# A decoder trunk on one core: the norms' sums on VectorE, the odd norm's row inside the first query, mixing behind the scores

## The chip, the core and the metric

The kernel runs on one core of a Trainium2 chip. The core has five engines that run side by side and meet through semaphores: TensorE (matmuls, written PE), VectorE (DVE), ScalarE (ACT), GpSimd (POOL) and SyncE (SP, which here only starts DMAs). The metric is the time of one execution on the device in microseconds; it is given as the median of several runs.

## The reference

A trunk of four pre-norm residual layers over 256 tokens of 1024 channels, in float32, and a final norm. Cut to what is computed:

```python
def rmsnorm(x, g):
    y = x * rsqrt(mean(x * x, axis=-1) + 1e-6)
    return y * g

def trunk(x):                                  # 1 x 256 tokens x 1024
    h = x
    # even layer: gated conv of width 3 (512 channels) beside pooling over 2/4/8/16 positions (512)
    h = h + even_mixer(rmsnorm(h, mix_g[0]))   # w_in 1024 x 2048, w_out 1024 x 1024
    h = h + conv_ffn(rmsnorm(h, ffn_g[0]))     # w_in 1024 x 5632, w_out 2816 x 1024
    # odd layer: 8 heads of forgetting attention, 8 of MoBA with a T5 bias; w_in 1024 x 3080, w_out 1024 x 1024
    h = h + odd_mixer(rmsnorm(h, mix_g[1]))
    h = h + conv_ffn(rmsnorm(h, ffn_g[1]))
    return rmsnorm(h, final_g)

def conv_ffn(h):
    u, g = split(h @ w_in)                     # 2816 each
    return (silu(causal_dwconv3(u) + b) * g) @ w_out
```

## The kernel before

**Layout.** Activations stand transposed: `h` is 128 partitions x 8 chunks of 1024 channels x 256 tokens. All weights are read once, in blocks of 128x1024 float32, by DMAs that SyncE starts into eight staging buffers `st`. A block is split into two parts of reduced precision: ScalarE casts `hi` (L141), VectorE subtracts and keeps `lo` (L142). The split blocks stand in rings of seven buffers, six blocks ahead of their use, so that the cast of a block waits until TensorE is through with the block seven before it. Every product is the sum of three: `hi` with `x_hi`, `hi` with `x_lo`, `lo` with `x_hi` (L290 to L292), or, in the FFN, one matmul of 512 columns (L314, both parts of `x` side by side) and one of 256 (L315).

**Stages.** Even layer, FFN 0, odd layer, FFN 1, final norm. A `boundary` between two layers (L383) closes the product in four blocks b=0..3, adds each to `h` (L381), and splits `h` times the norm's gain into `hg` (ScalarE L209, VectorE L210); the split has a high priority, since the next layer's first products read it. The norm's factor, one number per token, is multiplied in later, behind the products. For it `Stats.feed` squares each block of `h` (ScalarE L225, two buffers `sq`), GpSimd adds the squares up (`sqs` L230, `tot` L235), `columns` sums over partitions by two matmuls with ones into `pst` (L238), VectorE makes `var` of it (L252) and GpSimd raises it to -1/2 (`rcol` L254: a column, one number per partition). `rows` turns `rcol` by two transposes (L244) and ScalarE copies them as `rrow` (L247).

**FFN.** 22 chunks f of 128 channels. The in-product of f gives `zu` and `zg`; `added` copies them into `zs` (three buffers); `gate` multiplies with `rrow` (L549), does the convolution, the SiLU and the product `y` (L556), which is split into `y_h` and `y_l`. The out-product of f comes some chunks later, the last two of FFN 0 in the boundary behind it. For f=0 u and g alternate. `columns` stands between u and g of f=1; `rows`, with the gates of f=0 and 1 right behind it, between u and g of f=2.

**Odd layer.** `values(0)` makes the values of the first heads and the forget gates' inputs in four PSUM banks `pv` of the pool psA, all that it has, with `columns` ahead of the last chunk; ScalarE and VectorE scale them by `rcol` (`va` L642 and L643, `xg` L641). Then come `rows` and `rq`, and a loop over eight pairs of heads i: queries of i (`zq`, 24 matmuls, and in their middle `turn(i-2)`, six transposes of the probabilities `pr`), `score(i-1)` (12 matmuls of 64 rows, `ps_s`), keys of i (`zk`, 24 matmuls, and in their middle `mix(i-2)`, four matmuls of 64 columns into `po`). VectorE makes logits `lg` of the scores, ScalarE the exponentials, VectorE divides (L732 to L734); `po` is split into `yoh` and `yol`. Behind the loop stand the out-products `odd_add`, 24 matmuls each, among which the last pairs are turned, scored and mixed.

**What sets the order.** TensorE's order is that of the program. ScalarE's and VectorE's is fixed too when the program is built, by a scheduler that goes by priorities, except in the start and in the final norm, where it is that of the program. Each engine takes its instructions strictly in that order.

## Time and profile before

| | |
|---|---|
| median of 3 runs | 576.18 us (575.69 to 576.53) |
| profiled execution | 576.41 us, its span 574.7 us |
| mean granted clock of TensorE | 0.995 |
| busy: TensorE, VectorE, ScalarE, GpSimd | 98%, 78%, 60%, 11% |

The span is what the trace covers, from the first instruction to the last; 1.7 us of the profiled execution lie around it. A row of a timeline has the start, the time of its instructions taken together (neighbours that read alike are one row, with their count behind an x), the engine, the line, and in brackets how long the engine stood idle ahead of it and what it waited for. TensorE's matmuls overlap: what one costs is the distance between two starts, not the time in its row.

### The profile page before, as it was taken

How to read it: one execution, taken by the hardware profiler on the slowest of the kernel's cores; microseconds unless marked ns; L12 is line 12 of the kernel's file. 1: busy time of each engine (PE TensorE's matmuls, PEld its weight loads, DVE VectorE, ACT ScalarE, POOL GpSimd, SP SyncE). 2: the span in 40 equal slices, each digit the busy share in tenths (PEclk: the TensorE clock that was granted, in tenths of full speed). 3: DMA queues.
4: the chain of work that ended last, by engine and by line, in shares of the span. 5: the costliest groups of instructions: out<-in, count | busy, mean ns of one | idle time of the engine just before them, and what ended most of it. 6: DMA issues, size and time to landing. Idle time of an engine off the chain costs nothing.

```text
span 574.7 us, 9941 instructions
## 1 busy us (share of the span) xinstructions
PE 563.5 (98%) x3774; PEld 510.9 (89%) x3774; DVE 449.8 (78%) x776; ACT 346.0 (60%) x611; POOL 64.7 (11%) x81
## 2 busy tenths in 40 slices
PE   8999999999999999999899999999999999999995
PEld 7999988999999999999889999998888888888883
DVE  6999697987788778779648888488977778887752
ACT  6764476665655555557557666566755556555532
POOL 1542031000000000004001335031000000000000
PEclk9999999999999999999899999999999999999999
DMA  8965736566566656654665543437556655655001
GB/s 307 404 234 198 251 106 219 195 210 186 184 188 192 198 185 187 190 182 134 226 194 167 194 130 120 159 112 257 174 192 182 188 192 182 200 181 196 2 0 74
DMA packets 30080, 104.44 MB, mean 182 GB/s; under 512 B 3632, under 2 KB 3904, under 8 KB 30032
## 3 DMA queue, kind: packets, MB, share of 16 engines
q1 hardware_dynamic: 28944, 100.87, 53.9%
q0 software_dynamic: 944, 2.68, 1.6%
q8 instruction: 29, 0.48, 0.3%
q10 hardware_dynamic: 144, 0.26, 0.1%
q14 instruction: 19, 0.16, 0.1%
HBM read 102.73 MB, written 1.07 MB: 181 GB/s over the span
## 4 chain that ended last, share of the span: by engine, by line
PE 57%; issue 34%; DVE 4%; ACT 2%; POOL 2%; DMA 1%; SPq 0%; POOLq 0%; ACTq 0%; DVEq 0%
PE zu L314 8%; PE zg L314 7%; PE zu L315 4%; PE zg L315 4%; PE ta L291 3%; PE ta L290 3%; PE ta L292 3%; PE pv L633 2%; PE zk L290 2%; PE acc L290 2%; DVE lo L142 2%; PE acc L291 1%; PE acc L292 1%; PE zq L290 1%; PE zq L291 1%
## 5 line engine op out<-in xcount | busy, mean ns | idle before, releaser
L142 DVE TENSOR_TENSOR lo<-st,hi 128x1024 fp32r<-128x1024 f32 (+2 forms) x186 | 228.4, 1234 | 74.6 <-ACT hi L141 73.3
L141 ACT CAST hi<-st 128x1024 fp32r<-128x1024 f32 (+2 forms) x186 | 192.2, 1039 | 119.2 <-PE acc L291 32.1
L314 PE MATMUL zu<-hg,hi 128*128 128x512 f32 x352 | 125.6, 394 | 0.6 <-DVE hg L210 0.6
L314 PE MATMUL zg<-hg,hi 128*128 128x512 f32 x352 | 125.6, 394 | 0.0
L315 PE MATMUL zu<-hg,lo 128*128 128x256 f32 x352 | 98.6, 280 | 0.0
L315 PE MATMUL zg<-hg,lo 128*128 128x256 f32 x352 | 98.5, 280 | 0.0
L314 PEld LDWEIGHTS zu<-hg,hi 128*128 128x128 f32 x352 | 66.1, 188 | 15.9 <-DVE hg L210 1.3
L314 PEld LDWEIGHTS zg<-hg,hi 128*128 128x128 f32 x352 | 66.2, 188 | 14.9
L315 PEld LDWEIGHTS zu<-hg,lo 128*128 128x128 f32 x352 | 66.2, 188 | 0.7
L315 PEld LDWEIGHTS zg<-hg,lo 128*128 128x128 f32 x352 | 66.2, 188 | 0.0
L291 PE MATMUL acc<-y_l,hi 128*128 128x256 f32 x176 | 49.5, 281 | 0.0
L290 PE MATMUL acc<-y_h,hi 128*128 128x256 f32 x176 | 49.5, 281 | 0.0
L292 PE MATMUL acc<-y_h,lo 128*128 128x256 f32 x176 | 49.3, 280 | 0.0
L323 ACT CAST y_h<-y 128x256 fp32r<-128x256 f32 x44 | 17.7, 406 | 39.6 <-DVE y L556 39.6
L291 PE MATMUL ta<-lo,y_h 128*128 128x512 f32 x88 | 34.7, 394 | 0.0
L290 PE MATMUL ta<-hi,y_h 128*128 128x512 f32 x88 | 34.7, 394 | 0.0
L292 PE MATMUL ta<-hi,y_l 128*128 128x512 f32 x88 | 34.5, 393 | 0.0
L290 PEld LDWEIGHTS acc<-y_h,hi 128*128 128x128 f32 x176 | 33.1, 188 | 0.8
L291 PEld LDWEIGHTS acc<-y_l,hi 128*128 128x128 f32 x176 | 33.3, 189 | 0.0
L292 PEld LDWEIGHTS acc<-y_h,lo 128*128 128x128 f32 x176 | 33.2, 188 | 0.0
L401 ACT ACTIVATE t<-zs,vec 128x256 f32<-128x256 f32 x44 | 26.4, 600 | 11.0 <-DVE zs L549 10.9
L549 DVE TENSOR_TENSOR zs<-zs,rrow 128x512 f32<-128x512 f32 x44 | 30.2, 691 | 1.2
(217 smaller groups left out, 1160.6 us busy)
## 6 DMA issues: line engine op xcount, KB each, us to landing
st<-in_ff_in SPq DMA_DIRECT2D x88, 512.0 KB, 4.1
st<-in_ff_out SPq DMA_DIRECT2D x44, 512.0 KB, 4.3
st<-in_od_qk SPq DMA_DIRECT2D x16, 512.0 KB, 4.5
st<-in_ev_in SPq DMA_DIRECT2D x10, 512.0 KB, 7.4
st<-in_ev_out SPq DMA_DIRECT2D x8, 512.0 KB, 4.3
st<-in_od_out SPq DMA_DIRECT2D x8, 512.0 KB, 3.4
first<-in_first SPq DMA_DIRECT2D x7, 388.0 KB, 6.5
st<-in_od_vf SPq DMA_DIRECT2D x4, 520.0 KB, 3.6
```

The lines of the kernel that those rows point to most:

```text
L141: nc.scalar.copy(hi[:, s:e], st[:, s:e])
L142: nc.vector.tensor_sub(lo[:, s:e], st[:, s:e], hi.bitcast(F32)[:, s:e])
L290: nc.tensor.matmul(o, wh, xh, start=start, stop=False, skip_group_check=skip)
L291: nc.tensor.matmul(o, wh, xl, start=False, stop=False, skip_group_check=skip)
L292: nc.tensor.matmul(o, wl, xh, start=False, stop=stop, skip_group_check=skip)
L314: nc.tensor.matmul(z, wh, x[:, k], start=first, stop=False, skip_group_check=True)
L315: nc.tensor.matmul(z[:, 1, :], wl, x[:, k, 0, :], start=False, stop=last, skip_group_check=True)
L323: nc.scalar.copy(hi, src)
L401: nc.scalar.activation(t, u, AF.Identity, scale=col(w0 + 2), bias=bias)
L549: nc.vector.tensor_mul(zs, zs, rrow[:, None, :].to_broadcast([P, 2, T]))
L633: nc.tensor.matmul(o[:, :e - s], x[y], w[z][:, kk * c + s:kk * c + e], start=k == y == z == 0, stop=k == NK - 1 and y == 1)
```

## The change

- The sums of squares, `sqs` (three per norm) and `tot`, go from GpSimd to VectorE, in all four norms that have them.
- In the FFN `columns` stands behind g of f=1, and `rows` with the two gates behind g of f=2.
- In the odd layer `rows` and `rq` go into the middle of the first pair's query product.
- `mix(i-2)` stands right behind `score(i-1)`, and the keys' 24 matmuls run on without a break. In the tail `odd_add(1)` stands ahead of the last score.
- At the start the dummy operand of the warming matmuls is one column, broadcast; one of the first DMAs is started by ScalarE's queue, and ScalarE's first square comes behind it.
- In the final norm the division by 1024 goes into the squares' scale, and ScalarE's half of the first output (`send_left(0)`) stands behind the square of the last product.

```diff
--- before.py
+++ after.py
@@ -173,11 +173,11 @@
     place = {b[0]: i for i, b in enumerate(blocks)}
 
 
-    dummy = const.tile([P, T], F32, name="dummy")
+    dummy = const.tile([P, 1], F32, name="dummy")
     nc.vector.memset(dummy, 0.0)
     pw_ = psA.tile([P, 512], F32, tag="ps", name="pwarm")
     for _ in range(WARM):
-        nc.tensor.matmul(pw_[:, :T], dummy[:, :P], dummy, start=True, stop=True)
+        nc.tensor.matmul(pw_[:, :T], dummy.to_broadcast([P, P]), dummy.to_broadcast([P, T]), start=True, stop=True)
     vec = const.tile([P, V_N], F32, name="vec")
     ident = const.tile([P, P], F32, name="ident")
     make_identity(nc, ident)
@@ -211,8 +211,6 @@
                                        op0=ALU.mult, op1=ALU.subtract)
 
     hg = new_hg()
-    warm = const.tile([P, 1], F32, name="warm")
-    nc.scalar.activation(warm, ones, AF.Square)
     class Stats:
 
 
@@ -227,12 +225,12 @@
                 self.sum = sq
             else:
                 s = nrm.tile([P, 2, T], F32, tag="sqs", name="sqs")
-                nc.gpsimd.tensor_add(s, self.sum, sq)
+                nc.vector.tensor_add(s, self.sum, sq)
                 self.sum = s
 
         def columns(self, ps):
             tot = nrm.tile([P, T], F32, tag="tot", name="tot", bufs=1)
-            nc.gpsimd.tensor_add(tot, self.sum[:, 0, :], self.sum[:, 1, :])
+            nc.vector.tensor_add(tot, self.sum[:, 0, :], self.sum[:, 1, :])
             self.p = ps.tile([P, 512], F32, tag="ps", name="pst")
             for i in range(2):
                 nc.tensor.matmul(self.p[:, i:i + 1], tot[:, i * P:(i + 1) * P], ones, start=True, stop=True)
@@ -265,7 +263,9 @@
     rc = const.tile([P, PAD], F32, name="rc")
     for k in range(NK):
         for s, e in ((0, LEAD + T), (LEAD + T, FIRST)) if k == 0 else ((0, FIRST),):
-            nc.sync.dma_start(first[:, k, s:e], a["first"][k, :, s:e])
+            (nc.scalar if s else nc.sync).dma_start(first[:, k, s:e], a["first"][k, :, s:e])
+    warm = const.tile([P, 1], F32, name="warm")
+    nc.scalar.activation(warm, ones, AF.Square)
     st = Stats()
     with tc.manual_schedule(engines={mybir.EngineType.Activation, mybir.EngineType.DVE}):
         for k in range(NK):
@@ -576,12 +576,12 @@
                 for c in range(2):
                     for k in range(NK):
                         in_halves(z[c], (wu, wg)[c], k, hg[2], k == 0, k == NK - 1)
-                    if f == 1 and c == 0:
+                    if f == 1 and c == 1:
                         st.columns(ps_acc)
-                    if f == 2 and c == 0:
-                        rrow = st.rows()
-                        for b in range(2):
-                            gate(b, (early, zs)[b])
+                if f == 2:
+                    rrow = st.rows()
+                    for b in range(2):
+                        gate(b, (early, zs)[b])
                 zs = added(z)
                 if f >= 2:
                     gate(f, zs)
@@ -647,9 +647,6 @@
 
         xg = odc.tile([P, 2, NH], F32, name="xg")
         values(0)
-        rrow = st.rows()
-        rq = odc.tile([P, T], F32, name="rq")
-        nc.vector.tensor_scalar(rq, rrow, -(HD ** -0.5), None, op0=ALU.mult)
         ab = odc.tile([P, 2, NH], F32, name="ab")
         nc.vector.scalar_tensor_tensor(ab, xg, -1.0, xg, op0=ALU.mult, op1=ALU.max)
         nc.scalar.activation(ab, ab, AF.Exp, scale=-1.0)
@@ -756,12 +753,18 @@
             ready[p] = split(od, po[:, :T], None, "yo", bufs=8)
 
         ready = {}
+        rows = {}
+
+        def norm_rows():
+            rows["k"] = st.rows()
+            rows["q"] = odc.tile([P, T], F32, name="rq")
+            nc.vector.tensor_scalar(rows["q"], rows["k"], -(HD ** -0.5), None, op0=ALU.mult)
 
         def queries(p, between=None):
             z = psA.tile([P, 512], F32, tag="ps", name="zq")
             in_chunk(z[:, :T], weights(("q", p)), hg, between)
             qf = od.tile([P, T], F32, tag="qf", name="qf")
-            nc.vector.tensor_mul(qf, z[:, :T], rq)
+            nc.vector.tensor_mul(qf, z[:, :T], rows["q"])
             ahead()
             return split(od, qf, None, "qs")
 
@@ -769,9 +772,10 @@
             z = psA.tile([P, 512], F32, tag="ps", name="zk")
             in_chunk(z[:, :T], weights(("k", p)), hg, between)
             kf = od.tile([P, T], F32, tag="kf", name="kf")
-            nc.vector.tensor_mul(kf, z[:, :T], rrow)
+            nc.vector.tensor_mul(kf, z[:, :T], rows["k"])
             ahead()
             return split(od, kf, None, "ks")
+
 
 
         qs, ks, pr, pb, turned = {}, {}, {}, {}, {}
@@ -789,10 +793,11 @@
 
         for i, p in enumerate(order):
             pb[i] = bias_of(p)
-            qs[i] = queries(p, lambda: turn_at(i - 2))
+            qs[i] = queries(p, (lambda: turn_at(i - 2)) if i else norm_rows)
             if i >= 1:
                 score(i - 1)
-            ks[i] = keys(p, lambda: mix_at(i - 2))
+            mix_at(i - 2)
+            ks[i] = keys(p)
             if i == 0:
                 f_columns()
                 values(1)
@@ -804,8 +809,8 @@
 
         odd_add(0)
         turn_at(NPAIR - 2)
+        odd_add(1)
         score(NPAIR - 1)
-        odd_add(1)
         mix_at(NPAIR - 2)
         odd_add(2)
         turn_at(NPAIR - 1)
@@ -833,26 +838,32 @@
             def products(i, n):
                 for m, (w, y) in enumerate(tail):
                     acc.add(i, n, w, y, m == len(tail) - 1)
-                nc.scalar.activation(junk, acc.t[i][n], AF.Square, accum_out=sums[:, i, n:n + 1])
+
+                nc.scalar.activation(junk, acc.t[i][n], AF.Square, scale=D ** -0.5, accum_out=sums[:, i, n:n + 1])
                 if n == 0:
                     nc.vector.tensor_mul(hg_[:, i, :], acc.t[i][0], gb[:, :512])
-                    nc.vector.tensor_scalar(var[:, i:i + 1], sums[:, i, 0:1], 1.0 / D, EPS, op0=ALU.mult, op1=ALU.add)
-
-            def send(i, queue):
-                r, v = rcol[:, i:i + 1], var[:, i:i + 1]
-                nc.vector.scalar_tensor_tensor(v, sums[:, i, 1:2], 1.0 / D, v, op0=ALU.mult, op1=ALU.add)
+                    nc.vector.tensor_scalar(var[:, i:i + 1], sums[:, i, 0:1], EPS, None, op0=ALU.add)
+
+            def send_right(i):
+                r = rcol[:, i:i + 1]
+                v = var[:, i:i + 1]
+                nc.vector.tensor_add(v, sums[:, i, 1:2], v)
                 nc.gpsimd.tensor_tensor(r, v, mhalf[:, 0:1], op=ALU.pow)
                 nc.vector.scalar_tensor_tensor(o[:, i, 512:], acc.t[i][1], r, gb[:, 512:], op0=ALU.mult, op1=ALU.mult)
-                nc.scalar.activation(o[:, i, :512], hg_[:, i, :], AF.Copy, scale=r)
+                nc.sync.dma_start(out[i, :, 512:], o[:, i, 512:])
+
+            def send_left(i, queue):
+                nc.scalar.activation(o[:, i, :512], hg_[:, i, :], AF.Copy, scale=rcol[:, i:i + 1])
                 queue.dma_start(out[i, :, :512], o[:, i, :512])
-                nc.sync.dma_start(out[i, :, 512:], o[:, i, 512:])
 
             products(0, 0)
             products(0, 1)
             products(1, 0)
-            send(0, nc.sync)
+            send_right(0)
             products(1, 1)
-            send(1, nc.scalar)
+            send_left(0, nc.sync)
+            send_right(1)
+            send_left(1, nc.scalar)
 
     def ordered_final(acc, tail):
         with tc.manual_schedule(engines={mybir.EngineType.Activation, mybir.EngineType.DVE}):
```

**VectorE at the odd norm,** from the third block's sum on. `h` is the boundary's sum, `hg` the split, `lo` a weight block's, `var` the norm's. Before:

```order
L381 TENSOR_TENSOR h<-acc_1487,h 128x512
L210 SCALAR_TENSOR_TENSOR hg<-h,vec,hg 128x256 x2
L381 TENSOR_TENSOR h<-acc_1488,h 128x512
L210 SCALAR_TENSOR_TENSOR hg<-h,vec,hg 128x256 x4
L142 TENSOR_TENSOR lo_3285<-st_3283,hi_3284 128x1024
L142 TENSOR_TENSOR lo_3331<-st_3329,hi_3330 128x1024
L142 TENSOR_TENSOR lo_3361<-st_3359,hi_3360 128x1024
L142 TENSOR_TENSOR lo_3391<-st_3389,hi_3390 128x1024
L142 TENSOR_TENSOR lo_3430<-st_3428,hi_3429 128x1024
L252 TENSOR_SCALAR var<-pst 128x2
```

After, from the last block's split on:

```order
L210 SCALAR_TENSOR_TENSOR hg<-h,vec,hg 128x256 x2
L228 TENSOR_TENSOR sqs<-sq 128x512
L210 SCALAR_TENSOR_TENSOR hg<-h,vec,hg 128x256 x2
L142 TENSOR_TENSOR lo_3285<-st_3283,hi_3284 128x1024
L228 TENSOR_TENSOR sqs<-sqs,sq 128x512
L142 TENSOR_TENSOR lo_3331<-st_3329,hi_3330 128x1024
L228 TENSOR_TENSOR sqs<-sqs,sq 128x512
L142 TENSOR_TENSOR lo_3361<-st_3359,hi_3360 128x1024
L142 TENSOR_TENSOR lo_3391<-st_3389,hi_3390 128x1024
L233 TENSOR_TENSOR tot<-sqs 128x256
L142 TENSOR_TENSOR lo_3430<-st_3428,hi_3429 128x1024
L250 TENSOR_SCALAR var<-pst 128x2
```

The first sum stands between the last two pairs of `hg`, the two others and `tot` among the weight splits; `var` stays behind the fifth split. The boundaries ahead of the two FFNs have their sums in the same places among fewer splits.

**VectorE at the end of FFN 0.** `zs` belongs to the last chunk, f=21, `y` and `y_l` are its result. Before:

```order
L545 TENSOR_TENSOR zs<-zg,zb 128x256
L549 TENSOR_TENSOR zs<-zs,rrow 128x512
L142 TENSOR_TENSOR lo_3130<-st_3128,hi_3129 128x1040
L404 SCALAR_TENSOR_TENSOR t<-zs,vec,t 128x255
L405 SCALAR_TENSOR_TENSOR t<-zs,vec,t 128x254
L142 TENSOR_TENSOR lo_3160<-st_3158,hi_3159 128x1040
L556 TENSOR_TENSOR y<-s,zs 128x256
L329 TENSOR_TENSOR y_l<-y,y_h 128x256
```

After:

```order
L545 TENSOR_TENSOR zs<-zu,zb 128x256
L142 TENSOR_TENSOR lo_3100<-st_3098,hi_3099 128x1040
L142 TENSOR_TENSOR lo_3130<-st_3128,hi_3129 128x1040
L545 TENSOR_TENSOR zs<-zg,zb 128x256
L549 TENSOR_TENSOR zs<-zs,rrow 128x512
L142 TENSOR_TENSOR lo_3160<-st_3158,hi_3159 128x1040
L404 SCALAR_TENSOR_TENSOR t<-zs,vec,t 128x255
L405 SCALAR_TENSOR_TENSOR t<-zs,vec,t 128x254
L142 TENSOR_TENSOR lo_3190<-st_3188,hi_3189 128x1040
L556 TENSOR_TENSOR y<-s,zs 128x256
L329 TENSOR_TENSOR y_l<-y,y_h 128x256
```

Four splits now stand between the copy of `zu` and `y`, where two stood, and the last chunk's `y` comes behind the split of block 3190.

**VectorE in the odd layer's tail,** at the last score. `ksl` is the last pair's keys, `lg` its logits. Before:

```order
L329 TENSOR_TENSOR ksl<-kf,ksh 128x256
L142 TENSOR_TENSOR lo_4825<-st_4823,hi_4824 128x1024
L720 ISA lg,mx<-ps_s_4629,nb 128x256
L720 ISA mx 128x1
L722 ISA lg,mx<-ps_s_4629,nb 128x128
```

After:

```order
L329 TENSOR_TENSOR ksl<-kf,ksh 128x256
L142 TENSOR_TENSOR lo_4825<-st_4823,hi_4824 128x1024
L142 TENSOR_TENSOR lo_4914<-st_4912,hi_4913 128x1024
L717 ISA lg,mx<-ps_s_4653,nb 128x256
L717 ISA mx 128x1
L719 ISA lg,mx<-ps_s_4653,nb 128x128
```

One more split, of block 4914, stands ahead of the logits.

## Rows read from the trace of the kernel before

**Rows 1.** The page: busy time, share of the span and instructions of each engine.

```profile
PE 563.5 (98%) x3774; PEld 510.9 (89%) x3774; DVE 449.8 (78%) x776; ACT 346.0 (60%) x611; POOL 64.7 (11%) x81
```

**Rows 2.** TensorE's list of waits: us in total, times, longest.

```profile
PE pst L244 <- POOL rcol L254: 1.5, 1, 1.5
...
PE zx L480 <- DVE lo L281: 0.4, 2, 0.2
```

**Rows 3.** Timeline of TensorE, first FFN: start us, us, engine line op, [idle before <-releaser].

```profile
81.01 0.28 PE L315 MATMUL zg<-hg,lo 128*128 128x256 f32 x1
81.70 0.50 PE L314 MATMUL zu<-hg,hi 128*128 128x512 f32 x1 [0.41 <-DVE hg L210]
82.05 0.28 PE L315 MATMUL zu<-hg,lo 128*128 128x256 f32 x1
```

**Rows 4.** Timeline of VectorE, the boundary ahead of the first FFN.

```profile
75.02 0.69 DVE L381 TENSOR_TENSOR h<-acc,first 128x512 f32<-128x512 f32 x1
75.63 0.88 DVE L210 SCALAR_TENSOR_TENSOR hg<-h,vec,hg 128x256 fp32r<-128x256 f32 x2
...
78.88 2.77 DVE L210 SCALAR_TENSOR_TENSOR hg<-h,vec,hg 128x256 fp32r<-128x256 f32 x2 [0.42 <-ACT hg L209]
```

**Rows 5.** Timeline of GpSimd, the same boundary.

```profile
78.54 1.29 POOL L230 TENSOR_TENSOR sqs<-sqs,sq 128x512 f32<-128x512 f32 x1 [0.22 <-ACT sq L225]
```

**Rows 6.** Timeline of TensorE, start of the second FFN.

```profile
386.00 0.50 PE L314 MATMUL zu<-hg,hi 128*128 128x512 f32 x1 [0.23 <-DVE hg L210]
```

**Rows 7.** Timelines of TensorE, then VectorE, last products of the first FFN.

```profile
240.56 0.28 PE L290 MATMUL acc<-y_h,hi 128*128 128x256 f32 x1
...
243.37 0.39 PE L314 MATMUL zu<-hg,hi 128*128 128x512 f32 x1
...
249.41 0.42 DVE L329 TENSOR_TENSOR y_l<-y,y_h 128x256 fp32r<-128x256 f32 x1
```

**Rows 8.** Timeline of VectorE, odd norm.

```profile
265.77 3.98 DVE L210 SCALAR_TENSOR_TENSOR hg<-h,vec,hg 128x256 fp32r<-128x256 f32 x2 [0.42 <-ACT hg L209]
269.68 6.30 DVE L142 TENSOR_TENSOR lo<-st,hi 128x1024 fp32r<-128x1024 f32 x5
275.91 0.14 DVE L252 TENSOR_SCALAR var<-pst 128x2 f32<-128x2 f32 x1
```

**Rows 9.** Timeline of GpSimd, odd norm.

```profile
276.13 0.72 POOL L254 TENSOR_TENSOR rcol<-var,mhalf 128x2 f32<-128x2 f32 x1 [5.77 <-DVE var L252]
```

**Rows 10.** Timeline of TensorE, last values and first query.

```profile
274.96 0.41 PE L633 MATMUL pv<-hi,hg 128*128 128x264 f32 x2
...
277.41 0.39 PE L290 MATMUL zq<-hg,hi 128*128 128x256 f32 x1
```

**Rows 11.** Windows of both: PE, PEld, DVE, ACT, POOL busy, PEclk, DMA share, GB/s.

```profile
78.00:84.00 6.00, 5.58 (x33) 4.67 (x32) 5.58 (x6) 5.41 (x10) 3.89 (x6) 1.00 0.03 1
278.50:282.10 3.60, 3.60 (x20) 3.60 (x19) 0.46 (x2) 3.55 (x5) 0.00 (x0) 0.53 0.71 277
```

**Rows 12.** Timeline of TensorE, transposes of the first FFN.

```profile
91.33 0.38 PE L244 MATMUL pst<-ident,rcol 128*128 128x128 f32 x2
```

**Rows 13.** Timelines of TensorE and VectorE, one round of the loop over head pairs.

```profile
334.44 0.28 PE L292 MATMUL zk<-hg,lo 128*128 128x256 f32 x1
334.65 0.66 PE L754 MATMUL po<-ptb,va 128*64 128x256 f32 x4
...
336.29 0.17 DVE L732 RECIPROCAL rs<-sm 128x2 f32<-128x2 f32 x1 [0.35 <-ACT pr L727]
```

**Rows 14.** Timeline of VectorE, tail of the odd layer.

```profile
358.87 0.42 DVE L720 CUSTOM_DVE_ANT_0 lg<-ps_s,nb 128x256 f32<-128x256 f32 x1
...
361.76 0.28 DVE L734 TENSOR_SCALAR pr<-pr,rs 128x128 f32<-128x128 f32 x1
```

**Rows 15.** Timelines of TensorE and ScalarE, the end.

```profile
567.15 0.39 PE L292 MATMUL ta<-hi,y_l 128*128 128x512 f32 x1
...
568.38 0.58 ACT L836 ACTIVATE junk<-ta 128x512 f32<-128x512 f32 x1
```

## The prediction

> **What bounds the kernel now.** I read the page first: TensorE is busy 98% of the span, VectorE 78%, ScalarE 60%, GpSimd 11% [rows 1]. So time can be won only where TensorE stands still, runs slowly, or restarts. The list of its waits came next: most of it is one wait for GpSimd's `rcol` in the odd norm, beside small ones at the start [rows 2]. Then I followed the timelines of TensorE at the norms and, at each of its holes, those of the engine it waited for; last the windows of single stretches, where the granted clock is low behind the odd norm and full behind the smaller holes [rows 11]. Most of the change (sums, gates, the order of mixing) is in work off TensorE, and is worth only what these holes give back.
>
> **Part 1, sums on VectorE: the two boundaries into the FFNs.** Between 81.01 and 82.05 TensorE starts one 512- and one 256-column matmul, for 1.04 us; the same pair takes 0.35 elsewhere (from 240.56 to 243.37 there are 24 matmuls of 256 columns, so 0.117 each [rows 7], and a 512-column one is twice that). 0.69 us is lost, 0.41 of it marked as waiting for `hg` of VectorE [rows 3]. VectorE's pair of `hg` costs 0.88 us where GpSimd is still, and 2.77 at the last block [rows 4], while GpSimd adds the squares at 78.54 for 1.29 us [rows 5]. Both read two operands from SBUF. The change gives these adds to VectorE: 128x512, like the 0.69 us add of L381 [rows 4], so three and a half that size cost about 2.4 us; the two adds behind the last pair stand among weight splits that have time. Only the first stands ahead of the last `hg` pair (order, first fences). That pair, which starts at 78.88 now, is then done by about 79.8 (78.88 + 0.88) at the latest, where TensorE wants it at 81. The stall goes: **-0.69**. What is late next there is a weight cast, whose buffer is free by then: nothing.
> The second boundary shows the same with 0.23 marked [rows 6] and the same restart (0.28 beyond the marked wait, from rows 3): **-0.51**. If the slow pair had another cause both terms are zero or worse (rival 3).
>
> **Part 2, the gates of the FFNs moved.** The columns and rows have cover: two whole in-products, 5.6 us each (16 pairs of 0.35), lie between the gates and the first product with `y`, and the gates of f=0 and f=1 move by half of one. But the change shifts VectorE's pattern by one f: it alternates between an early `y` and one behind two more weight splits, and the late kind now falls on the last f (order, second fences). Before, the late kind was at f=20: its in-product ended at 240.56, and `y_l` was done at 249.83, 9.27 us later [rows 7]. The boundary wants `y_l` after three out-products of 2.81 us and 0.35 to 0.47 of the closing, at 8.9 us. **+0.37**, between 0 (if ScalarE or the splits come earlier) and 0.6. The second FFN ends with the final's own order and has 1.7 us of slack: nothing.
>
> **Part 3, the odd norm.** Before, a last pair of `hg` takes 3.98 us beside GpSimd, five splits queue behind it to 275.91, and `var`, though its columns are in PSUM by then, waits for them; `rcol` takes 0.72 us more [rows 8, 9]. The values' last matmuls start at 274.96 and are through at about 275.20; the first query starts at 277.41 [rows 10], 2.2 us later, transposes among it. Then from 278.5 to 282.1 the granted clock is 0.53, close to the lower level of 1.2 GHz [rows 11]: of the window's 20 matmuls three reach in from its edges, and 17 take 3.5 us instead of 17 x 0.117 = 2.0, 1.5 us more.
> After, the pair takes 0.9, the sums 2.4, so the first four splits end no later, and the fifth is bound by its cast, which waits for TensorE: done at about 274.3. The chain from `var` to the query takes 277.41 - 275.91 = 1.50 us and stays, for the query's PSUM bank is one of the four that the values fill, and a bank is free only after the scaling by `rcol`. So the query starts at 275.8, and 0.6 us of hole stays, 1.6 less than before. The transposes go into the middle of the query; two of them take 0.38 us among other matmuls at 91.33 [rows 12], of which I take 0.2 as added (0 to 0.38). Does the clock fall? The hole of 0.69 us at 81 left it at 1.00 (the window from 78 to 84), while 2.2 us came before the fall [rows 11]. The new hole is much nearer the small ones, so I take no fall: -1.6 + 0.2 - 1.5 = **-2.9**. Bounds: -0.5 (the fall stays, `rcol` takes 1 us more) to -3.3.
> The Trainium skill ("TensorE: Matmul & The Clock Gate", Part 4: PE-mode transpose) speaks against this: transposes don't count as activity as matmuls do. By that rule two transposes in the middle of the query, right behind a hole, would bring the low clock back, which is rival 1; the trace has them between full-speed matmuls at 91.33, without a fall.
>
> **Part 4, mixing behind the scores.** In the loop over eight head pairs TensorE changes four times per round between full-width products, 64-row scores and 64-column mixes; now three times, in six rounds. The first mix matmul starts 0.21 us after the last key matmul instead of 0.117 [rows 13], 0.09 for the entry, and I take the same for the pipe's first matmul behind a change: 0.1 to 0.2 per change, so 0.6 to 1.2 in six rounds; I take **-0.95** (bounds 0.0 to -1.4). ScalarE's `yoh` and VectorE's `yol` (a 128x256 step of 0.42, as in rows 7) move in front of the softmax's division, where VectorE now waits 0.35 us [rows 13]: it all but fits.
>
> **Part 5, the tail of the odd layer.** The last score moves behind `odd_add(1)`, and on VectorE one more split, whose cast waits for that product, goes ahead of the last softmax (order, third fences). From the softmax's first step to its last takes 358.87 to 362.04, 3.17 us [rows 14]. With S the start of score(7): cast to S+1.1, split to S+2.3, softmax done at S+5.5. TensorE has 12 score matmuls (0.84), four mixes (0.8), 24 matmuls (2.9) and the first three transposes ahead of the ones that need it: S+4.9. **+0.5**, between 0 and 0.8. Before, no such split stood there and `pr` was there in time.
>
> **Part 6, start and end.** At the start less stands on SP and VectorE ahead of the first data, but the DMAs bound it; two waits of 0.2 each show what can be won [rows 2]. Against that the even norm's sums stand behind weight splits and may delay the columns by 0.2. **-0.1** (-0.5 to +0.4). At the end the last square runs at 568.38, 0.84 us after the last matmul (567.15 + 0.39), since ScalarE does `o` of the first half ahead of it [rows 15]; in the new order it comes first: **-0.55** (-0.3 to -0.6).
>
> **Sum.** -0.69 - 0.51 + 0.37 - 2.9 - 0.95 + 0.5 - 0.1 - 0.55 = -4.8 us. From the profiled 576.41 us that is 571.6; the median of the runs before is 0.23 below the profiled one, so **571.4**.
>
> **The rivals.** *1: the low clock stays in the first query.* For it: the hole is not zero, and the page's rule on transposes; against it: the full clock behind the holes at 81 and 386 [rows 6, 11]. Price +1.5: 572.9. *2: the mix gains nothing,* since scores and mixes are both half-sized forms and the change between them costs as much as two, or the split before the softmax no longer fits VectorE's wait of 0.35 us: +0.95, 572.3. *3, slower: the slow `hg` pairs are not GpSimd's doing.* Place: VectorE at three boundaries. Then the pair stays at 2.8 to 4.0 us and one add comes in front: both FFN boundaries cost 0.6 more than now instead of giving 1.2 (+2.4), and in the odd norm the 2.4 us of sums push `var` to 278.3, so the hole grows by 2.4 instead of shrinking by 1.6, and the clock falls (+5.5). In all 571.4 + 7.9 = 579.3. It decides from where the sums cost VectorE more than the pairs give back: 2.4 us against 3.1 in the odd norm, 1.9 and more at the others. Against it: the pair is 0.88 in the same boundary just before GpSimd starts. *4: the change does less than it says:* another late part, say `rcol` at twice its time, keeps half of the odd norm's hole and the clock's fall: +2.3, 573.7.
>
> **How the numbers follow.** Forecast 0.55, rival 1 0.17, rival 2 0.12, rival 4 0.10, rival 3 0.06. A difference under 0.2% (1.15 us) can't be told from none in this kernel. All but rival 3 lie 2.5 us or more below 576.18; some of rival 4 with a missing gain elsewhere would come within 0.2%: faster 0.91, same 0.04, slower 0.05. The range goes from 569.8 (mixing at -1.4, no loss at the FFN's end and the tail: -1.3 and a little) to 573.7 (rival 4).
>
> **What would show it.** Right: the last `hg` pair under 1.8 us at all three boundaries and no marked wait at 81 and 386; `var` at about 274.3, the query at 275.8, clock 1.00 to 282; a wait of some 0.4 for `y_l` near 258 and of 0.5 for `pr` near 362; three jumps a round in the loop; the last square right at the end of the last matmul. Wrong: a low clock behind the odd norm, a longer pair of `hg`, or waits for `pr` in every round, which at 0.8 us in six rounds would eat the whole gain.

## The result, and the profile after

The changed kernel takes 570.88 us (median of 4 runs, 570.48 to 572.0) where the kernel before takes 575.93 (4 runs, 574.58 to 576.53): a ratio of 0.9919, 95% interval 0.9896 to 0.9941. The forecast was 571.4, between 569.8 and 573.7. The profiled execution after took 570.93 us, its span 569.2 against 574.7.

The runs of the kernel before fall into two groups by TensorE's mean granted clock: of 47 later runs 19 stand at 0.994 or 0.995, with a median of 576.0 us, and 28 at 0.996 or more, with 574.5. The profile shown ahead of the prediction is one of the first group, and the experiments below deal with this.

Where the 5.5 us of span went, read at starts of the same matmuls in both traces:

| start of | before | after | difference | step since the row above |
|---|---|---|---|---|
| columns of the even norm (L238) | 23.35 | 22.78 | -0.57 | start: -0.57 |
| values of the odd layer (first L633) | 263.21 | 262.42 | -0.79 | first FFN boundary -0.69, end of FFN 0 +0.34, others +0.13 |
| first query | 277.41 | 275.03 | -2.38 | hole of the odd norm: -1.59 |
| first keys | 281.70 | 278.19 | -3.51 | clock -1.37, transposes inside +0.24 |
| out-products of the odd layer | 353.74 | 349.04 | -4.70 | clock's rest in the keys -0.16, mixing -1.03 |
| product behind the last turn | 365.46 | 361.19 | -4.27 | tail: +0.43 |
| last products of FFN 1 (L360) | 409.79 | 404.94 | -4.85 | second FFN boundary: -0.58 |
| end of the span | 574.7 | 569.2 | -5.5 | end: -0.65 |

The clock's term is counted in the trace of before: from 278.57 to 281.70 it has 15 of the query's matmuls, about 0.21 us apart where 0.117 is usual. The page's busy line after, then two lines of TensorE's list of waits (us in total, times, longest):

```profile
PE 560.7 (99%) x3774; PEld 509.7 (90%) x3774; DVE 445.3 (78%) x792; ACT 346.5 (61%) x611; POOL 46.0 (8%) x65
```

```profile
PE zq L290 <- ACT va L643: 0.4, 1, 0.4
PE ps_t L738 <- DVE pr L731: 0.3, 1, 0.3
```

Beside these the list has only the wait at the very start. No wait for `hg` is left, and none for `rcol`; the two shown are the remainder in the odd norm and the new one in the tail. VectorE at the boundary ahead of the first FFN, after, against [rows 4]:

```profile
77.26 0.68 DVE L228 TENSOR_TENSOR sqs<-sq 128x512 f32<-128x512 f32 x1
78.02 0.88 DVE L210 SCALAR_TENSOR_TENSOR hg<-h,vec,hg 128x256 fp32r<-128x256 f32 x2
78.82 1.22 DVE L142 TENSOR_TENSOR lo<-st,hi 128x1024 fp32r<-128x1024 f32 x1
```

The first sum takes 0.68 us, the last pair of `hg` 0.88 instead of 2.77. The odd norm after, VectorE, ScalarE, TensorE, and the window of [rows 11] (PE, PEld, DVE, ACT, POOL busy, PEclk, DMA share, GB/s), against [rows 8 to 11]:

```profile
264.63 0.87 DVE L210 SCALAR_TENSOR_TENSOR hg<-h,vec,hg 128x256 fp32r<-128x256 f32 x2
...
272.37 1.23 DVE L142 TENSOR_TENSOR lo<-st,hi 128x1024 fp32r<-128x1024 f32 x1 [0.79 <-ACT hi L141]
273.51 0.15 DVE L250 TENSOR_SCALAR var<-pst 128x2 f32<-128x2 f32 x1
...
274.50 0.47 ACT L643 ACTIVATE va<-pv,rcol 128x256 f32<-128x256 f32 x1 [2.16 <-PE pv L633]
...
274.18 0.41 PE L633 MATMUL pv<-hi,hg 128*128 128x264 f32 x2
275.03 0.38 PE L290 MATMUL zq<-hg,hi 128*128 128x256 f32 x1 [0.44 <-ACT va L643]
...
278.50:282.10 3.60, 3.60 (x31) 3.56 (x30) 2.25 (x5) 3.59 (x6) 0.00 (x0) 1.00 0.02 5
```

`var` comes 2.40 us earlier, behind a fifth split that starts only when its cast is there; the query still waits for `va`, 0.6 us behind the last values, and the clock is 1.00.

The end of FFN 0 after: VectorE's late `y`, TensorE's first product with `y_l` and the page's group of its weight loads (busy, mean ns, idle before, releaser):

```profile
254.56 1.24 DVE L142 TENSOR_TENSOR lo<-st,hi 128x1040 fp32r<-128x1040 f32 x1 [0.67 <-ACT hi L141]
255.72 0.42 DVE L556 TENSOR_TENSOR y<-s,zs 128x256 f32<-128x256 f32 x1
256.61 0.42 DVE L329 TENSOR_TENSOR y_l<-y,y_h 128x256 fp32r<-128x256 f32 x1 [0.47 <-ACT y_h L323]
...
256.63 0.39 PE L290 MATMUL acc<-y_h,hi 128*128 128x256 f32 x1
257.09 0.38 PE L291 MATMUL acc<-y_l,hi 128*128 128x256 f32 x1
...
L291 PEld LDWEIGHTS acc<-y_l,hi 128*128 128x128 f32 x176 | 33.3, 189 | 0.3 <-DVE y_l L329 0.3
```

256.63 to 257.09 is 0.46 for a step of 0.117: the wait for `y_l`. The tail after, VectorE and TensorE, against [rows 14]: the split ahead of `lg`, the last step of `pr`, and the transpose that waits for it:

```profile
356.51 1.22 DVE L142 TENSOR_TENSOR lo<-st,hi 128x1024 fp32r<-128x1024 f32 x1 [2.27 <-ACT hi L141]
357.65 0.42 DVE L717 CUSTOM_DVE_ANT_0 lg<-ps_s,nb 128x256 f32<-128x256 f32 x1
...
360.55 0.28 DVE L731 TENSOR_SCALAR pr<-pr,rs 128x128 f32<-128x128 f32 x1
...
360.88 0.33 PE L738 MATMUL ps_t<-ident,pr 128*128 128x128 f32 x1 [0.27 <-DVE pr L731]
```

And the end, TensorE and ScalarE, against [rows 15]: the square follows the last matmul by 0.1 us (562.30 + 0.39 = 562.69), `o` comes behind it.

```profile
562.30 0.39 PE L292 MATMUL ta<-hi,y_l 128*128 128x512 f32 x1
...
562.79 0.60 ACT L842 ACTIVATE junk<-ta 128x512 f32<-128x512 f32 x1 [1.39 <-PE ta L292]
...
563.37 0.71 ACT L856 ACTIVATE o<-hg__6749,rcol 128x512 f32<-128x512 f32 x1
```

### The profile page after: what moved, and what is told of

Read it like the earlier page. It is cut to its first block, busy times and chain, and to the rows that moved or that the text cites. A ratio compares the mean times of both kernels' runs of the same rounds, so it can differ in the third digit from the quotient of the medians.

```text
span 569.2 us, 9949 instructions
## 1 busy us (share of the span) xinstructions
PE 560.7 (99%) x3774; PEld 509.7 (90%) x3774; DVE 445.3 (78%) x792; ACT 346.5 (61%) x611; POOL 46.0 (8%) x65
## 4 chain that ended last, share of the span: by engine, by line
PE 94%; ACT 2%; DVE 1%; DMA 1%; issue 1%; SPq 0%; POOLq 0%; POOL 0%; ACTq 0%; DVEq 0%
PE zu L314 14%; PE zg L314 14%; PE zu L315 7%; PE zg L315 7%; PE acc L291 6%; PE acc L290 6%; PE acc L292 6%; PE pv L633 4%; PE ta L291 3%; PE ta L290 3%; PE ta L292 3%; PE zk L290 1%; PE zq L290 1%; PE zk L291 1%; PE zq L291 1%; PE zk L292 1%
## 5 line engine op out<-in xcount | busy, mean ns | idle before, releaser
L142 DVE TENSOR_TENSOR lo<-st,hi 128x1024 fp32r<-128x1024 f32 (+2 forms) x186 | 224.6, 1210 | 74.1 <-ACT hi L141 72.6
```

The source lines that it names most:

```text
L142: nc.vector.tensor_sub(lo[:, s:e], st[:, s:e], hi.bitcast(F32)[:, s:e])
```

## The experiments

All are edits of the changed kernel.

**1. What the sums on VectorE are worth.** The sums back on GpSimd:

```diff
-                nc.vector.tensor_add(s, self.sum, sq)
+                nc.gpsimd.tensor_add(s, self.sum, sq)
-            nc.vector.tensor_add(tot, self.sum[:, 0, :], self.sum[:, 1, :])
+            nc.gpsimd.tensor_add(tot, self.sum[:, 0, :], self.sum[:, 1, :])
```

> The changed kernel with one part undone: the sums of squares on GpSimd again, all else as changed. Theory (GpSimd's adds slow VectorE's last pairs of hg and hold the squares' buffers): the last pair takes 2.6 us or more at the two FFN boundaries and about 4 in the odd norm, TensorE waits 0.4 and 0.2 for hg again (+0.7 and +0.5 us with the restart), var comes near 275 and the first query's hole is about 2 us, behind which the clock falls (+1.6 and +1.5): about 575 us, 4.2 above the changed kernel. Rival (the gain of the odd norm came from the moved transposes): the pairs may slow down, but hole and clock stay good, and the time is at most 1.5 above, 572.

574.01 us, median of 10 runs; ratio to the kernel before 0.9983 (0.9970 to 0.9997). So of the 5 us some 3 hang on the sums. The profile (573.61 us) shows the places; VectorE at the first FFN and in the odd norm, TensorE, and the window behind:

```profile
78.32 2.77 DVE L210 SCALAR_TENSOR_TENSOR hg<-h,vec,hg 128x256 fp32r<-128x256 f32 x2 [0.42 <-ACT hg L209]
...
265.68 3.97 DVE L210 SCALAR_TENSOR_TENSOR hg<-h,vec,hg 128x256 fp32r<-128x256 f32 x2 [0.42 <-ACT hg L209]
...
277.30 0.39 PE L290 MATMUL zq<-hg,hi 128*128 128x256 f32 x1 [1.97 <-ACT va L643]
...
276.50:282.50 6.00, 5.20 (x44) 5.20 (x45) 1.34 (x6) 5.66 (x10) 0.24 (x1) 1.00 0.71 258
```

Slow pairs and hole are back as in [rows 4, 8], gaps of 0.57 and 0.39 us in TensorE's starts at the FFNs too. But in this profile the clock stays at 1.00 behind a hole of 2.1 us, which the theory had not expected: the result is 1 us below it.

**2. Is it GpSimd's adding itself?** Three adds at each boundary that nothing waits for:

```diff
             st.feed(b)
+            if b:
+                side = nrm.tile([P, 2, T], F32, tag="side", name="side", bufs=1)
+                nc.gpsimd.tensor_add(side, h[:, 2 * b:2 * b + 2, :], h[:, 2 * b:2 * b + 2, :])
```

> The changed kernel with three adds of 128x512 put on GpSimd at each boundary, h plus h into a buffer that nobody reads; the norm's sums stay on VectorE and nothing waits for the added work. Theory (the two engines get in each other's way when both read two operands from SBUF): VectorE's pairs of hg and its sums that fall beside an add of 1.3 us grow from 0.88 to 1.4 to 2.8 us, TensorE waits at one boundary or more, 0.5 to 3 us in all, with up to 1.5 more if the clock falls. Rival (the slow pairs came from the norm's own waits, through the squares' buffers and ScalarE): the pairs stay at 0.9 and the time at 571 within 0.3.

575.34 us (one run), 4.5 above the changed kernel. VectorE and GpSimd at the first FFN, then the second step of one pair of the odd boundary by itself, with the add beside it, and TensorE's columns of the odd norm:

```profile
73.49 1.66 DVE L210 SCALAR_TENSOR_TENSOR hg<-h,vec,hg 128x256 fp32r<-128x256 f32 x2
...
73.66 1.21 POOL L395 TENSOR_TENSOR side<-h 128x512 f32<-128x512 f32 x1 [18.32 <-DVE h L381]
...
263.86 1.26 DVE L210 SCALAR_TENSOR_TENSOR hg<-h,vec,hg 128x256 fp32r<-128x256 f32 x1
...
263.69 1.15 POOL L395 TENSOR_TENSOR side<-h 128x512 f32<-128x512 f32 x1 [1.03 <-DVE h L381]
...
274.92 0.58 PE L236 MATMUL pst<-ones,tot 128*128 128x1 f32 x4 [1.38 <-DVE tot L233]
```

Every pair of `hg` beside an add takes 1.65 instead of 0.87, nine times in three boundaries; the pair without one keeps 0.87. Nothing waits for `side`, so the squares' buffers have no part in it. VectorE gets 2.3 us late in the odd norm, and there `tot` is late for the columns. The rival falls. The second step of a pair starts in its place (263.86) but takes 1.26 instead of 0.48, and ends at 265.12, 0.28 us after the add (263.69 + 1.15 = 264.84). The kernel before shows the same distance. Two adds fall beside the long pair of [rows 4], that of [rows 5] and the next:

```profile
80.08 1.28 POOL L230 TENSOR_TENSOR sqs<-sqs,sq 128x512 f32<-128x512 f32 x1
```

That pair ends at 81.65 (78.88 + 2.77), 0.29 us after the second add (81.36). So in these rows a step that meets an add lasts until a little after the add's end, and two steps can meet two adds. The Trainium skill ("SBUF — State Buffer", Who interferes with whom) says that a VectorE instruction with two SBUF inputs contends with a GpSimd one that reads SBUF, and that the ports they share are an exclusive lock; these rows agree.

**3 and 4. How long may the hole be?** VectorE steps of 128x512 between columns and `var` in the odd norm, one and two:

```diff
...
+                for _ in range(late):
+                    nc.vector.scalar_tensor_tensor(src, self.sum, self.p[:, 0:1], self.sum, op0=ALU.mult, op1=ALU.add)
...
+                nc.vector.tensor_copy(src[:, 0:2], self.p[:, 0:2])
-            self.rcol = rstd(self.p)
+            self.rcol = rstd(src)
```

> The changed kernel with one VectorE step of 128x512 (about 0.7 us) put between the odd norm's columns and var, so that the first query starts later and TensorE's hole grows from 0.6 to about 1.4 us, with the two transposes still in the middle of the query. Theory (it is the hole's length that brings the clock down, and 0.6 is far from it): hole 1.4; the granted clock behind it is still 1.00, time +0.8; if it falls, +2.3. Rival (the transposes bring it down): the clock is full here as in the changed kernel, whatever the hole.

> The same with two such steps: hole about 2.1 us, as long as before the change, but without transposes in it. Theory (the hole's length decides): the granted clock falls to about 0.5 for three to four us behind it and the time is 1.5 + 1.5 = 3.0 us above the changed kernel, about 573.9. Rival (the transposes ahead of the query, or something else of the kernel before, brought it down): clock 1.00, time +1.5, about 572.4.

The holes came out longer than meant, 1.9 and 2.4 us beyond the usual step, times 572.0 and 573.1 (one run each). The clock was full behind both, as the rival of the second had it. TensorE and the window of the longer one:

```profile
274.58 0.41 PE L640 MATMUL pv<-hi,hg 128*128 128x264 f32 x2
277.21 0.38 PE L297 MATMUL zq<-hg,hi 128*128 128x256 f32 x1 [2.23 <-ACT va L650]
...
276.50:282.50 6.00, 5.29 (x45) 5.29 (x46) 2.08 (x7) 5.76 (x11) 0.15 (x1) 1.00 0.44 154
```

That is a longer hole than the one ahead of the fall in [rows 11], so the theory that length alone decides falls. One profile each can't say more; 10 and 11 count runs.

**5. What moving the transposes is worth.** `rows` and `rq` ahead of the first query again:

```diff
         values(0)
...
+        rows["k"] = st.rows()
+        nc.vector.tensor_scalar(rows["q"], rows["k"], -(HD ** -0.5), None, op0=ALU.mult)
...
-            qs[i] = queries(p, (lambda: turn_at(i - 2)) if i else norm_rows)
+            qs[i] = queries(p, lambda: turn_at(i - 2))
```

> The changed kernel with the transposes and rq of the odd norm ahead of the first query again, all else as changed. Theory (the first query waits for a PSUM bank that is free only after the scaling by rcol, so the transposes were hidden ahead of it, and moving them cost 0.2 us): the query starts within 0.15 us of 275.0, the keys behind it start 0.2 earlier than in the changed kernel, time 0.2 us less or the same. Rival (the moved transposes shortened the hole): the query starts 0.4 us later and the time is 0.3 us more.

570.51 us (one run). The query starts at 274.81, in a run that is 0.22 us earlier from the even norm's columns on, so at the same point; the keys come 2.90 us behind it instead of 3.16, 0.26 less:

```profile
274.30 0.43 PE L242 MATMUL pst<-ident,rcol 128*128 128x128 f32 x2
274.81 0.38 PE L290 MATMUL zq<-hg,hi 128*128 128x256 f32 x1
```

The theory holds: ahead of the query the transposes are hidden by the wait for the bank, inside it they cost some 0.25 us. This part of the change won nothing by itself; in 9, where the query has another bank, it lets the query start before `rcol` is turned.

**6. What mixing behind the scores is worth.**

```diff
-            mix_at(i - 2)
-            ks[i] = keys(p)
+            ks[i] = keys(p, lambda: mix_at(i - 2))
```

> The changed kernel with mix(i-2) in the middle of the keys again, all else as changed. Theory (each change between full-width and half-sized matmuls costs some 0.16 us, one fewer per round): from the first mix to the tail TensorE needs 1.0 us more than in the changed kernel, with no marked wait in either. Rival (the order of VectorE and ScalarE made the gain, by an earlier pr): waits for pr or ptb show up in the rounds.

571.61 us (one run). Between the first query and the first out-product TensorE needs 1.06 us more (0.67 late there, 0.39 early ahead of it), no wait is added. TensorE behind one score and around the mix here, then around one mix in the changed kernel, where the score's last matmuls are ahead of it:

```profile
328.80 0.28 PE L712 MATMUL ps_s<-ksh,qsl 64*128 64x128 f32 x2
329.01 0.39 PE L290 MATMUL zk<-hg,hi 128*128 128x256 f32 x1
329.23 0.28 PE L291 MATMUL zk<-hg,hi 128*128 128x256 f32 x1
...
330.41 0.28 PE L292 MATMUL zk<-hg,lo 128*128 128x256 f32 x1
330.62 0.66 PE L751 MATMUL po<-ptb,va 128*64 128x256 f32 x4
...
331.43 0.39 PE L290 MATMUL zk<-hg,hi 128*128 128x256 f32 x1
331.65 0.28 PE L291 MATMUL zk<-hg,hi 128*128 128x256 f32 x1
```

```profile
328.67 0.28 PE L712 MATMUL ps_s<-ksh,qsl 64*128 64x128 f32 x2
328.87 0.66 PE L751 MATMUL po<-ptb,va 128*64 128x256 f32 x4
...
329.68 0.39 PE L290 MATMUL zk<-hg,hi 128*128 128x256 f32 x1
329.90 0.28 PE L291 MATMUL zk<-hg,hi 128*128 128x256 f32 x1
```

The step into the mix is 0.2 us from the keys (330.41 to 330.62) and from the last two scores (328.67 to 328.87) alike, and the way back into the keys is the same in both, 0.22 us from their first matmul to the next. What is saved is the change from the scores to the keys, which this kernel has beside the others: 0.21 us behind its last two scores and 0.22 to the second key, where 0.11 to 0.12 is usual, some 0.2 us a round.

**7. Three places mended.** The last score ahead of `odd_add(1)`, FFN columns, rows and gates between u and g again, and for the first query a bank of psB:

```diff
-            z = psA.tile([P, 512], F32, tag="ps", name="zq")
+            z = (psA if p != order[0] else psB).tile([P, 512], F32, tag="ps", name="zq")
...
-        odd_add(1)
         score(NPAIR - 1)
+        odd_add(1)
...
-                    if f == 1 and c == 1:
+                    if f == 1 and c == 0:
                         st.columns(ps_acc)
-                if f == 2:
+                    if f == 2 and c == 0:
...
```

> The changed kernel with three things mended: the last score ahead of odd_add(1) again, the columns, rows and gates of the FFNs between u and g again, and the first query's result in a bank of psB, which is free, so that it need not wait for the scaling of the values. Theory: no wait for pr near 361 (-0.45), none for y_l near 257 (-0.35), no hole ahead of the first query (-0.6): 1.4 us below the changed kernel, about 569.5. Rival for each: the columns between u and g wait for the sums on VectorE (+0.3 to +1), the bank in psB is wanted by the forget gates' products (+0.5), and the time is within 0.3 of the changed kernel.

570.9 us (6 runs), ratio to the kernel before 0.9926 (0.9912 to 0.9940): the same as the changed kernel beside it (next). The three waits are gone in its profile, but, as the first rival had it, TensorE's columns now wait for `tot`, here and at 384.78:

```profile
84.14 0.28 PE L315 MATMUL zu<-hg,lo 128*128 128x256 f32 x1
84.94 0.58 PE L236 MATMUL pst<-ones,tot 128*128 128x1 f32 x4 [0.52 <-DVE tot L233]
```

The step into the columns is 0.68 us too long here and 0.60 there, 1.28 us in the two FFNs: the sums on VectorE are late for columns that stand this early, so the change had to move them.

**8. The changed kernel again.**

> The changed kernel once more, for its spread beside the others on the same chip. Theory (the low clock behind the odd norm comes in some runs of the kernel before and in none or few of this one): runs at 570.5 to 571.0 with a mean granted clock of 0.997 or more, fewer than 2 in 10 at 0.995 or less. Rival (the fall is as frequent): about half of the runs at 0.995 and 1.5 us longer.

571.12 us (6 runs, 570.27 to 571.65), ratio 0.9932 (0.9920 to 0.9944). With the 4 runs of the result none of 10 is at a granted clock of 0.995 or less; two are at 0.996.

**9. Columns late, rows and gates early.** As 7, with the columns behind g of f=1 as in the change:

```diff
                     if f == 1 and c == 1:
                         st.columns(ps_acc)
-                if f == 2:
+                    if f == 2 and c == 0:
...
```

> As the kernel with the three things mended, but with the columns behind g of f=1 as in the changed kernel, so that they need not wait for the sums, and only rows and gates between u and g of f=2. Theory (the mended places gave 1.4 us in their profile and the early columns took 1.3 back): no wait for tot at 84 and 384, the mended places as before, about 569.5, 1.4 below the changed kernel's 570.9. Rival (rcol is not ready for the transposes in the middle of f=2): a wait of up to 0.8 us at 89 and 389 and no gain.

569.13 us (4 runs, 568.95 to 569.45), ratio to the kernel before 0.9900 (0.9883 to 0.9918), the fastest here and, by the ratios, 0.3% below the changed kernel in 8. No marked wait is left in TensorE's list but the one at the very start. Its first query follows the values without a hole:

```profile
273.36 0.40 PE L633 MATMUL pv<-hi,hg 128*128 128x264 f32 x2
273.60 0.28 PE L290 MATMUL zq<-hg,hi 128*128 128x256 f32 x1
```

**10 and 11. What brings the clock down.** The sums on GpSimd make the long hole again; 10 has the transposes ahead of the query, in the hole, as the kernel before, 11 inside the query (the same kernel as 1).

```diff
 10: the edits of 1 and of 5
 11: the edit of 1
```

> Sums on GpSimd and the transposes ahead of the first query, which makes the odd norm that of the kernel before, in the changed kernel. Theory (the fall of the clock is an accident of the long hole, whatever stands in it): as many runs with a granted clock of 0.995 or less as with the sums back alone, some 3 in 10, time 574.0 in the others. Rival (the transposes inside the hole are what brings the clock down, as they stood there before): about half of the runs at 0.995 or less and near 575.5, as in the kernel before, where 11 of 24 runs show it.

> The sums on GpSimd again with the transposes inside the first query, once more, to be counted beside the one with the transposes ahead. Theory: runs at 573.6 to 574.3 with a clock of 0.997 or more, and some 3 in 10 at 0.995 or less and 1.5 us longer, as with the transposes ahead. Rival: none or 1 in 10 at 0.995 or less.

Of 10's 12 runs (median 573.84) one has a clock of 0.995 or less; of 11's 12 (573.93) five, and with 1's runs 6 of 22. Both were caught in it by their profile; the windows of 10 and 11:

```profile
276.50:282.50 6.00, 5.93 (x37) 5.68 (x37) 1.64 (x6) 5.94 (x12) 0.00 (x0) 0.72 0.62 227
```

```profile
276.50:282.50 6.00, 5.14 (x30) 5.14 (x31) 0.84 (x5) 4.99 (x10) 0.30 (x1) 0.72 0.68 247
```

From 278 to 280 the clock reads 0.50 in both, its lower level. So the fall comes with the transposes in the hole and without; the rival is not borne out. The 1 of 12 is fewer than 10's theory or its rival expected. It comes in some runs and not in others of one and the same kernel: 19 of 47 (the kernel before), 6 of 22 (1 and 11) and 1 of 12 (10) with a hole of about 2 us, none of 20 in the kernels with a hole of 0.6 or none (the changed kernel, 7 and 9). The line at 0.995 is a rough one: three of 9's four runs are at 0.996, though its profile shows no fall here, and one run of 1 at 0.996 is as long (575.83) as those with the fall. What decides it in a single run isn't settled.

**12. The start.** The start of the kernel before (the warming matmuls' operands and the place of ScalarE's first square, not printed, go back too):

```diff
-    dummy = const.tile([P, 1], F32, name="dummy")
+    dummy = const.tile([P, T], F32, name="dummy")
...
-            (nc.scalar if s else nc.sync).dma_start(first[:, k, s:e], a["first"][k, :, s:e])
+            nc.sync.dma_start(first[:, k, s:e], a["first"][k, :, s:e])
```

> The changed kernel with the start of the kernel before (dummy of 256 columns, all first DMAs on SyncE, ScalarE's square ahead of them). The even norm's columns stood at 23.35 in the kernel before and at 22.4 to 23.2 in seven profiles with the changed start. Theory (the changed start is worth 0.3 to 0.5 us, its spread is that of the first DMAs): columns at 23.2 or later. Rival (the start is worth nothing): columns within 22.4 to 23.0.

571.54 us (one run), the columns at 23.37, as the theory had it:

```profile
23.37 0.50 PE L238 MATMUL pst<-ones,tot 128*128 128x1 f32 x4
```

With the new start twelve profiles have them at 22.4 to 23.2 (mean 22.7), with the old one two at 23.35 and 23.37: worth 0.2 to 1.0 us in single runs, about 0.6 in the mean. In every one of them the first warming matmul starts at 0.97 or 0.98 with the small dummy and at 1.24 with the large one. How the 0.6 divides between the three edits of the start isn't shown.

## Why the prediction was right, point by point

- **The FFN boundaries** (-0.69, -0.51): -0.69 and -0.58. Both shown by 1, and the cause by 2: the adds hold VectorE up whoever wants them.
- **The gates** (+0.37): +0.34, the wait for `y_l`, and it goes in 7 and 9 when the gates go back.
- **The odd norm** (-2.9): -2.9 in these two profiles, but of two different kinds. The shorter hole (-1.6) and the transposes inside (+0.24) are in every profile of the changed odd norm and are shown by 1 and 5. The clock's 1.5 us is the step that was wrongly reasoned: the prediction took the fall as the consequence of 2.2 us of hole, and it comes in about 4 of 10 runs of the kernel before. Against a run without it the change is worth 574.5 - 570.9 = 3.6 us, against one with it 5.1; the forecast of 571.4 held because the new hole never had it, as was said, not because of the rule it was said by. That the forecast started from a profile with the fall, and that three of the result's four runs before had it too, by their times, is luck: 1.5 of its 4.8 us hang on that draw. Rival 1, with the Trainium skill's rule ("TensorE: Matmul & The Clock Gate", Part 4: PE-mode transpose), found no support: in the kernel before the window from 91 to 97 us, with the two of [rows 12] in it, reads 1.00, with two transposes in the middle of the query none of 10 runs of the changed kernel shows a fall, and with the long hole 1 of 12 runs falls with the transposes in it, 6 of 22 with them in the query.
- **Mixing** (-0.95): -1.03, and 1.06 in 6; the mechanism as told, one change fewer per round. Rival 2 (scores to mixes cost as much as two changes, or the split delays the softmax) is refuted by 6: a step of 0.20, and no wait for `pr` in the rounds.
- **The tail** (+0.5): +0.43; it goes in 7 and 9.
- **The start** (-0.1): -0.57, the one term that was mis-sized, just outside its bounds. It was bounded by the two marked waits of 0.2, which leave out the one at the very start (1.2 us before, 1.0 after), and lowered by a cost of the sums that did not come; 12 shows 0.6. It makes up most of the 0.7 us by which the two profiles differ more than the sum.
- **The end** (-0.55): -0.65.
- **Rival 4** (another late part): the chain from `var` to the query takes 1.52 us (273.51 to 275.03) where 1.50 was forecast, and no late part shows.
- **Rival 3** (the slow pairs are not GpSimd's doing) is refuted by 1 and 2.

## What to carry to other kernels

Work on an idle engine isn't free: GpSimd's adds made VectorE's two-operand steps beside them three times as long and more (2.77 and 3.98 us a pair instead of 0.88). Look for instructions that take longer than their like, and for what runs beside them, before giving GpSimd the small sums. A change that moves work within a fixed order shifts whole patterns behind it; three of this one's side effects (the late `y`, the late last score, a bank that was still held) cost 1.4 us together and could be taken back one by one (569.1 us). And take a single profile's low clock as one draw: count it over runs before a forecast is built on it.

## What the runs showed of the hardware that was not expected

- A hole of 1.9 to 2.4 us in TensorE's work left the granted clock at 1.00 in the profiles of 1, 3 and 4, and a hole of 2.1 to 2.2 us brought it to about half for 3 to 4 us in those of the kernel before, of 10 and of 11, the last being the same program as 1. In the mean over a run this shows as 0.994 to 0.995, mostly, instead of 0.996 or more, and costs about 1.5 us.
- An add of 128x512 on GpSimd, 1.2 us long, costs VectorE's pair of 128x256 steps beside it 0.78 us each time, though nothing on VectorE waits for its result; the step that meets it ends about 0.28 us after the add.
- In experiment 2 the clock fell as well, behind a hole of 1.6 us ahead of the columns at 274.92; the columns and the values' last twelve matmuls followed, at 1.00 up to 276.8, and it fell there, ahead of the next hole of 0.5 us. A hole shorter than 2 us can thus stand before a fall, by one profile. The window (us, PE busy, PEclk, DMA share, GB/s):

```profile
276.80:277.00 0.20, 0.20 (x3) 0.53 1.23 430
```
